# Triangle products of two RWKV blocks placed inside later projection products, and the input's sums placed behind the last gate-up low part

## Chip, cores and metric

The kernel runs on one core of a Trainium2 chip. The metric is the device time of one execution in microseconds, the median of several runs. The core has five engines with a queue each: PE (matrix products), DVE (vector), ACT (scalar and activation), POOL and SP (which here mostly issue transfers). An instruction runs when those ahead of it on its engine are issued and what it waits for on other engines is done.

## What is computed

One layer of a hybrid decoder, for 512 prompt tokens and 8 x 4 sample tokens (544 columns in all, two halves of 272). It has a half-step SwiGLU feed-forward, a mixer with 8 RWKV-7 heads beside 4 differential-attention heads, and a second half-step feed-forward, each between two RMS norms:

```python
def layer(x, l, shift0, wkv0, attend, P):
    g = P['norm_gains'][l]
    h = x + 0.5 * rms_norm(swiglu(rms_norm(x, g[0], NORM_EPS), P['ff1_in'][l], P['ff1_out'][l]), g[1], NORM_EPS)
    m, k, v, wkv, shift = mixer(rms_norm(h, g[2], NORM_EPS), l, shift0, wkv0, attend, P)
    h = h + rms_norm(m, g[3], NORM_EPS)
    h = h + 0.5 * rms_norm(swiglu(rms_norm(h, g[4], NORM_EPS), P['ff2_in'][l], P['ff2_out'][l]), g[5], NORM_EPS)
    return h, k, v, wkv, shift

def swiglu(x, w_in, w_out):
    gate, up = jnp.split(x @ w_in, 2, axis=-1)
    return (jax.nn.silu(gate) * up) @ w_out

# inside mixer, the recurrence of the RWKV heads, one step:
    sa = jnp.einsum('bhvk,bhk->bhv', S, -kk_t)
    S = (S * w_t[:, :, None, :] + sa[..., None] * (kk_t * a_t)[:, :, None, :]
         + v_t[..., None] * k_t[:, :, None, :])
    return S, jnp.einsum('bhvk,bhk->bhv', S, r_t)
```

All matrices are float32. D_MODEL is 1024, D_FF 2816, a head has 64 columns.

## The kernel before

**Precision.** Each operand is split into a high and a low part (`whi`/`wlo` for weights, `xh`/`xl` and the like for activations), and a product is three matmuls: high by high, high by low, low by high. `dot` (L153) makes one product of 128 outputs: for k = 0 to 7 the two matmuls with the weight's high part (L162, L163), then eight with its low part (L168). Three accumulation banks are taken in turn by `acc_tile` (L198): two named `mm`, one `pb`. Other banks come from `abank` (three, L190) and `bank` (two, L184), all named `pb` in the trace.

**Order.** The program is written down in one order. A planner then gives every engine its own order: it takes an instruction when it expects its inputs and its room to be ready, and among the ready ones the one written first, or one under `high_priority`. `tc.issue_after(ins)` keeps the instructions of a block that run on the engine of `ins` behind `ins`. `after(None)` (L361) does nothing. A list `norm` holds small pieces of work: `dot` takes the first one from it behind its fourth k (L164), sets it behind the matmul just made, and sets the rest of the product behind the piece's last matmul (`last[0]`, L147 to L151).

**Feed-forward.** The 22 blocks of 128 hidden columns go in four groups (`GROUPS`). In the first group, gate and up products are plain; `hidden` (L460) applies SiLU on ACT, multiplies on DVE (L462) and calls `split` (L178): the high part on ACT (L180), the low part on DVE (L181). Then `products` (L387) makes the down products, for each m first the half s = 0, then s = 1; `finish` (L624) takes each result. The other groups use seven products instead of eight for a 2x2 block product (`seven`, L520). They need sums and differences of the four quarters of the scaled input: `mixtures` (L435), 16 steps, each an addition on DVE (L440, in place in `h`), a high part on ACT (L416) and a low part on DVE (L418). In the first group `finish` takes two of these steps per result (L627), so the first eight results carry all 16. The room of `h` is then given to the weights of the next groups (`wt`, L646): their loads (`t1`, L479; `b22`, L481) wait for the last of these steps, in SP's queue, in which the down weights (L129) are loaded too.

**RWKV blocks.** After the first feed-forward, the 8 heads go in four blocks of two (L889). Block 0 has its projections from `opening`; for blocks 1 to 3, `proj` (L748) makes six products at the top of the pass: k, r and v for s = 0, then for s = 1. The passes are written one behind another, but PE's work of a projection does not depend on the blocks before it. Each block then has a chain through all engines: `gates` (L876: products L143 to L145 into abank, sigmoid L885), token shift (L826), a scan (L903), exponentials (L905, L906), the norm of kk (`sums` L207, `inv_sqrt`, `spread` L254, L918), the bonus `bon` (L926, product L929, eviction L930), the g product (L938 with L143 to L145 into abank, eviction L939 into another tile named `bon`), and the parts of `cat`, whose part 1 is L944 and part 3 is L945 and L946. The chain ends with the triangle: per chunk of 64 tokens and head the 64 x 64 product of parts 1 and 3 (L957; 16 calls, 32 matmuls in the trace, as float32 operands take two) into one abank, masked into `ltm` on DVE (L958). `cat` is then stored (L960). `ltm` of all four blocks is read by the inversion behind the loop (L971), `cat` from DRAM by `ahead` (L1032).

Of the kernel before, what the change touches and what calls it, by code (L numbers as in the profile page):

```python
# [9 lines left out]
FT = mybir.dt.float32  # L10
# [3 lines left out]
OP = mybir.AluOpType  # L14
# [3 lines left out]
DM, DFF, SEQ, NB, DT = 1024, 2816, 512, 8, 4  # L18
# [9 lines left out]
NH, HD, CH = 8, 64, 64  # L28
NCH = SEQ // CH
# [23 lines left out]
def build(ctx, tc, A):  # L53
    nc = tc.nc
    V, S, G, T = nc.vector, nc.scalar, nc.gpsimd, nc.tensor
# [52 lines left out]
    ps = pa.tile([128, 512], FT, name="pb")  # L108
# [7 lines left out]
    C = {n: cst[:, o:o + w] for n, (o, w) in CST.items()}  # L116
# [61 lines left out]
    def split(pool, src, name, n=HALF, into=None, **kw):  # L178
        hi, lo = into or [pool.tile([128, n], FR, name=name + p, **kw) for p in "hl"]
        S.activation(hi, src, AF.Copy)  # L180
        V.tensor_tensor(lo, src, hi.bitcast(FT), op=OP.subtract)  # L181
        return hi, lo

    def bank():  # L184
# [5 lines left out]
    def abank():  # L190
        return pa.tile([128, 512], FT, name="pb")
# [1 line left out]
    def xbank():  # L193
        return px.tile([128, 512], FT, name="pb")

    turn, last, latest, root = [0], [None], [None], [None]

    def acc_tile():  # L198
        turn[0] += 1
# [104 lines left out]
    later, norm, ends, got = [], [], [], [None]  # L304
# [56 lines left out]
    def after(ins):  # L361
        return ExitStack() if ins is None else tc.issue_after(ins)
# [85 lines left out]
    def ff(win, wout, pre, h, done, xp, end, lead=None, begin=None, midway=None, ahead_of_end=None):  # L448
        with ExitStack() as st:
# [5 lines left out]
            sets, scaled, mixtures = combined(pre, h, fa, xp)  # L455
# [106 lines left out]
            for gi, (j0, j1) in enumerate(GROUPS):  # L562
                if gi == 0:
                    raw = [[gate_up() for _ in range(2)] for _ in range(2)]

                    def take(s, i, ps):
                        S.activation(raw[s][i // 2][i % 2], ps, AF.Copy)

                    if lead:
                        lead(take)  # L570
                        begin()
                    else:
                        opening([weights(win[j, i], 1024) for j in range(2) for i in range(2)], pre.xs, take, 2)

                    def scaled_raw(s):
                        for g, u in raw[s]:
                            V.tensor_tensor(g, g, pre.rs[s], op=OP.mult)
                            V.tensor_tensor(u, u, pre.rs[s], op=OP.mult)
                            hidden(s, g, u)

                    scaled_raw(0)
                    behind = [None, None]
                    for j in range(2, j1, 2):
                        if midway and j == 4:
                            midway()
                        ws = [[weights(win[i, n], 1024, added=begin is None and i == 3) for n in range(2)] for i in (j, j + 1)]
                        for s in range(2):
                            for both in ws:
                                pg, pu = acc_tile(), acc_tile()
                                for p, w in zip((pg, pu), both):  # L590
                                    dot(p, w, pre.xs[s])
                                if (j, s) == (2, 0) and both is ws[0]:
                                    scaled_raw(1)
                                g, u = gate_up()
                                V.tensor_tensor(g, pg, pre.rs[s], op=OP.mult)  # L595
                                V.tensor_tensor(u, pu, pre.rs[s], op=OP.mult)
                                hidden(s, g, u)
                                with after(j > 2 and behind[0] or None):
                                    for _ in range(4 * (j > 2)):
                                        next(scaled, None)  # L600
                                behind.append(made[0])
                                behind.pop(0)
                else:
                    for j in range(j0, j1):
                        now = ahead or seven(j)
                        if ahead is None:
                            next(now)
                        ahead = None
                        next(now)
                n = j1 - j0  # L610
                lastg = gi == len(GROUPS) - 1
                sqs = [Squares(0), Squares(1)]
                if lastg:
                    st1.close()
                    xp_stack.close()
                    end()
                    st2.close()
                    late = [None, (fa, 8), (fa, 8), (pool("wx"), 4)]
                elif gi:
                    ahead = seven(j1)  # L620
                    next(ahead)
                group, hid = hid, [[], []]

                def finish(s, m, ps):  # L624
                    if gi == 0:
                        S.activation(y[s][m], ps, AF.Copy)
                        for _ in range(2):  # L627
                            next(mixtures, None)
                    else:
                        with (tc.high_priority() if lastg and m >= KB - 2 else ExitStack()):  # L630
                            V.tensor_tensor(y[s][m], ps, y[s][m], op=OP.add)  # L631
                            if lastg and m == KB - 1:
                                sqs[s].finish(y[s][m])
                            elif lastg:
                                sqs[s].add(y[s][m])
                    if lastg and m == KB - 1:
                        done(s, y, sqs[s])
                    if lastg and ahead_of_end and (s, m) == (1, 1):
                        ahead_of_end()

                products(lambda m: wout[:, m, off:off + n * 128], group, y, finish, wx=late if lastg else None, apart=lastg)
                off += n * 128
                if gi == 0:
                    next(mixtures, None)
                    h_stack.close()
                    wt = pool("wt", st1, side="right")  # L646
# [139 lines left out]
    def projected(i):  # L786

        pr = pr_.tile([128, SEQ + 1 + NB * (DT + 1)], FT, name="pr", bufs=6)
        P, Q = pr[:, :SEQ + 1], pr[:, SEQ + 1:].rearrange("p (b t) -> p b t", t=DT + 1)
        G.memset(P[:, 0:1], 0.0)  # L790
        G.tensor_copy(Q[:, :, 0:1], shin[:, i, :].rearrange("p (b o) -> p b o", o=1))

        n = SEQ - HALF

        def take(s, ps, raw=False):
            for dst, src, r in (((P[:, 1:1 + HALF], ps, 0),) if s == 0 else
                                ((P[:, 1 + HALF:], ps[:, :n], slice(0, n)), (Q[:, :, 1:], bt(ps[:, n:]), slice(n, HALF)))):
                if raw:
                    S.activation(dst, src, AF.Copy)
                else:  # L800
                    scale(s, dst, src, r)

        def scale(s, dst, src, r):
            V.tensor_tensor(dst, src, rs[0] if s == 0 else (bt if len(dst.shape) == 3 else lambda a: a)(rs[1][:, r]),
                            op=OP.mult)

        def late_scale():
            scale(0, P[:, 1:1 + HALF], P[:, 1:1 + HALF], 0)
            scale(1, P[:, 1 + HALF:], P[:, 1 + HALF:], slice(0, n))
            scale(1, Q[:, :, 1:], Q[:, :, 1:], slice(n, HALF))  # L810

        late_scales[i] = late_scale

        return (12 + i, take), (i, P, Q)
# [19 lines left out]
    def c64(ap):  # L834
        return ap.rearrange("p (c t) -> p c t", t=CH)
# [40 lines left out]
    def gates(b):  # L876
# [9 lines left out]
            out.append(t)  # L886
        return out

    for b in range(4):  # L889
        cat = pp.tile([128, NCH, 5, CH], FT, name="cat", bufs=2)  # L890
        if b:
            items, new = zip(*(projected(i) for i in (4 + b, b, 8 + b)))
            proj(*items)
            prk, prr, prv = new
        else:
            prk, prr, prv = prs[2:5]
# [53 lines left out]
        V.tensor_tensor(ars[:, b, 1], r[:, SEQ:], cu[:, SEQ:], op=OP.mult)  # L950
        V.tensor_tensor(bt(ars[:, b, 0])[:, :, 1:], bt(kk[:, SEQ:])[:, :, 1:], bt(cu[:, SEQ:])[:, :, :DT - 1], op=OP.mult)
        V.tensor_copy(bt(ars[:, b, 0])[:, :, 0:1], bt(kk[:, SEQ:])[:, :, 0:1])
        ps = abank()
        for c in range(NCH):
            for e in range(2):
                rows = slice(e * HD, (e + 1) * HD)
                T.matmul(ps[rows, c * CH:(c + 1) * CH], cat[rows, c, 1, :], cat[rows, c, 3, :], start=True, stop=True)  # L957
        V.tensor_tensor(ltm[:, b * NCH:(b + 1) * NCH], c64(ps), C["lmask"].rearrange("p (o t) -> p o t", o=1).to_broadcast([128, NCH, CH]),  # L958
                        op=OP.mult)
        nc.sync.dma_start(cat_d[b], cat)  # L960
    nc.sync.dma_start(A["shifts"], shout)
    prep.close()
    ch2 = mix.enter_context(tc.tile_pool(name="ch2", bufs=1, reuse_waits="tile"))
# [725 lines left out]
```

## Time and profile before

| | us |
|---|---|
| runs (median; lowest to highest of 3) | 1194.22 (1191.49 to 1194.61) |
| the profiled execution | 1195.87 |
| its span, first to last instruction | 1194.1 |
| mean granted clock of PE | 0.988 of full speed |

All times of the trace come from the one profiled execution. Views used: the page of the profile; the list of who waited for whom; tables of stages (busy time of PE, PEld, DVE, ACT, POOL with instruction counts, then PEclk, the share of the DMA engines and GB/s); and the order of time of single engines. A row of the order of time has the start, the time, the engine, the line, the operation, output <- inputs, shapes and a count; in brackets the idle time of the engine just before, and who ended it. PE's matmuls overlap, so the step from one start to the next says more than the time of one. The first feed-forward takes the span up to about 405 us, the RWKV projections lie between 420 and 515, attention and the recurrence up to about 755, the second feed-forward behind that.

### The profile page before, as it was taken

The numbers are of one execution on the slowest core, as the hardware profiler recorded it, in microseconds if no ns is written. First come the engines' busy times: TensorE is split into PE (matmuls) and PEld (weight loads), VectorE is DVE, ScalarE is ACT, GpSimd is POOL, SyncE is SP. The second block draws the span as 40 slices with busy tenths as digits, with TensorE's granted clock in tenths as the row PEclk, the third lists the DMA queues.
The fourth block names the chain that finished last, engine by engine and source line by source line (L and its number), as shares of the span: only waits on it lengthen the run. The fifth ranks groups of instructions, "written<-read, shape, count | busy, mean of one in ns | idle before, by whom it ended". The sixth has DMA issues, their size and how long they took to land. (4 is left out here: it accounts for less than half of the span.)

```text
span 1194.1 us, 25487 instructions
## 1 busy us (share of the span) xinstructions
PE 1169.2 (98%) x10034; PEld 1105.7 (93%) x10034; DVE 814.4 (68%) x1878; ACT 585.0 (49%) x1083; POOL 169.3 (14%) x232
## 2 busy tenths in 40 slices
PE   9999999999999999999999999999999999999995
PEld 9999999999999999989887645999999999999995
DVE  7694674865876778678335657788784766757856
ACT  7455552633645665533114545567465634525530
POOL 0001210110101176421000031100001201101001
PEclk9999999999999999899899999999999999999998
DMA  8328884975756557689442487564259876857532
GB/s 270 104 89 240 208 208 123 214 181 136 168 201 177 138 147 209 218 233 235 117 144 85 142 291 274 162 189 133 69 151 230 213 180 150 209 152 182 116 116 75
DMA packets 88330, 205.42 MB, mean 172 GB/s; under 512 B 9209, under 2 KB 22905, under 8 KB 86803
## 3 DMA queue, kind: packets, MB, share of 16 engines
q1 hardware_dynamic: 67874, 148.64, 37.7%
q0 software_dynamic: 18032, 50.70, 23.8%
q10 hardware_dynamic: 2304, 4.46, 1.0%
q8 instruction: 79, 1.29, 0.4%
q14 instruction: 41, 0.33, 0.1%
HBM read 186.12 MB, written 18.95 MB: 172 GB/s over the span
## 5 line engine op out<-in xcount | busy, mean ns | idle before, releaser
L132 ACT ACTIVATE whi<-wraw 128x1024 fp32r<-128x1024 f32 (+2 forms) x125 | 114.8, 921 | 155.8 <-PE mm L163 76.8
L162 PE MATMUL mm<-xh,whi 128*128 128x272 f32 x440 | 115.4, 293 | 0.3 <-DVE ga L595 0.3
L163 PE MATMUL mm<-xl,whi 128*128 128x272 f32 x440 | 115.0, 292 | 0.0
L138 DVE TENSOR_TENSOR wlo<-wraw,whi 128x1024 fp32r<-128x1024 f32 (+2 forms) x98 | 98.0, 1002 | 20.2 <-ACT whi L132 13.9
L483 POOL DMA_DIRECT2D t<-in_ff_in_dram x32 | 38.8, 1213 | 335.3 <-DMA t<-in_ff_in_dram 155.5
L162 PEld LDWEIGHTS mm<-xh,whi 128*128 128x128 f32 x440 | 83.6, 190 | 1.2 <-DVE ga L595 0.6
L163 PEld LDWEIGHTS mm<-xl,whi 128*128 128x128 f32 x440 | 83.6, 190 | 0.3
L529 DVE TENSOR_TENSOR ga<-pb,ga 128x272 f32<-128x272 f32 x138 | 60.2, 436 | 22.8 <-PE pb L518 20.6
L168 PE MATMUL mm<-xh,wlo 128*128 128x272 f32 x440 | 66.5, 292 | 0.3 <-DMA wlo<-in_ff_in_dram 0.3
L515 PE MATMUL pb<-sh,t1h 128*128 128x272 f32 x256 | 66.7, 288 | 0.0
L516 PE MATMUL pb<-sl,t1h 128*128 128x272 f32 x256 | 66.6, 287 | 0.0
L495 ACT ACTIVATE t1h<-t 128x1024 fp32r<-128x1024 f32 x32 | 34.0, 1062 | 60.9 <-issue 35.9
L631 DVE TENSOR_TENSOR y<-mm,y 128x272 f32<-128x272 f32 x64 | 28.2, 440 | 51.9 <-PE mm L168 51.3
L163 PE MATMUL mm<-hd0l,whi 128*128 128x272 f32 x242 | 62.7, 288 | 0.0
L162 PE MATMUL mm<-hd0h,whi 128*128 128x272 f32 x242 | 62.5, 288 | 0.0
L168 PEld LDWEIGHTS mm<-xh,wlo 128*128 128x128 f32 x440 | 59.6, 190 | 0.9 <-DMA wlo<-in_ff_in_dram 0.5
L163 PE MATMUL mm<-hd1l,whi 128*128 128x272 f32 x232 | 60.2, 288 | 0.0
L162 PE MATMUL mm<-hd1h,whi 128*128 128x272 f32 x232 | 59.9, 289 | 0.0
L162 PE MATMUL pb<-xh,whi 128*128 128x272 f32 x216 | 56.9, 294 | 0.6 <-DVE vf L1113 0.6
L163 PE MATMUL pb<-xl,whi 128*128 128x272 f32 x216 | 56.7, 292 | 0.0
L515 PE MATMUL pb<-fa,whi 128*128 128x272 f32 x216 | 56.2, 288 | 0.0
L516 PE MATMUL pb<-fa,whi 128*128 128x272 f32 x216 | 56.2, 288 | 0.0
(495 smaller groups left out, 3662.8 us busy)
## 6 DMA issues: line engine op xcount, KB each, us to landing
wraw<-in_ff_in_dram SPq DMA_DIRECT2D x55, 512.0 KB, 4.6
wlo<-in_ff_in_dram POOLq DMA_DIRECT2D x34, 512.0 KB, 7.0
t<-in_ff_in_dram SPq DMA_DIRECT2D x64, 256.0 KB, 3.8
t<-in_ff_in_dram POOLq DMA_DIRECT2D x32, 512.0 KB, 5.9
wraw<-in_w_in_dram SPq DMA_DIRECT2D x26, 512.0 KB, 7.2
wlo<-in_w_in_dram POOLq DMA_DIRECT2D x25, 512.0 KB, 8.2
wraw<-in_ff_out_dram SPq DMA_DIRECT2D x32, 384.0 KB, 3.1
wraw<-in_ff_out_dram SPq DMA_DIRECT2D x32, 320.0 KB, 3.4
```

The source lines that it names most:

```text
L132: S.activation(hi, raw, AF.Copy)
L138: V.tensor_tensor(lo, raw, hi.bitcast(FT), op=OP.subtract)
L162: T.matmul(ps, hi, xs[k][0], start=k == 0, stop=False)
L163: latest[0] = T.matmul(ps, hi, xs[k][1], start=False, stop=False).ins
L168: latest[0] = T.matmul(ps, wcols(w, k0 + k)[1], xs[k][0], start=False, stop=k == n - 1).ins
L483: G.dma_start(t1, bass.AP(tensor=src.tensor, offset=src.offset, ap=[[1024, 128], [128 * 1024 + 512, 2], [1, 512]]), accum_op=OP.add)
L495: S.activation(hi, src, AF.Copy)
L515: T.matmul(ps, c, x[k][0], start=k == 0, stop=False)
L516: T.matmul(ps, c, x[k][1], start=False, stop=False)
L529: V.tensor_tensor(dst, p, q, op=op)
L631: V.tensor_tensor(y[s][m], ps, y[s][m], op=OP.add)
```

## The change

Two independent edits.

*The sums.* `split` notes its last low part in `lowest[0]`. In the first group's `finish`, the steps taken at m = 0 (four of 16) are as before; the DVE instructions of the other 12 are set behind the last low part, which is that of the last gate-up block of the half s = 1.

*The triangles.* A block's triangle becomes `triangle(i)`, for half i of its chunks: 8 calls into an abank of its own and a mask of half the size. For blocks 2 and 3 both halves stay where the triangle was, though behind the issue of the store of `cat`. For blocks 0 and 1 they go into `hooks`, four pieces, which the pass b = 2 gives to `norm` ahead of its `proj`: so the first four of the six products of the third block's projection take one half each behind their fourth k, blocks 0, 0, 1, 1 in order.

```diff
@@ split
-        V.tensor_tensor(lo, src, hi.bitcast(FT), op=OP.subtract)
+        lowest[0] = V.tensor_tensor(lo, src, hi.bitcast(FT), op=OP.subtract).ins
@@
-    turn, last, latest, root = [0], [None], [None], [None]
+    turn, last, latest, root, lowest = [0], [None], [None], [None], [None]
@@ finish
                         S.activation(y[s][m], ps, AF.Copy)
-                        for _ in range(2):
-                            next(mixtures, None)
+                        with after(lowest[0] if m else None):
+                            for _ in range(2):
+                                next(mixtures, None)
@@ the loop over blocks
+    hooks = []
     for b in range(4):
         cat = pp.tile([128, NCH, 5, CH], FT, name="cat", bufs=2)
         if b:
+            if b > 1:
+                norm.extend(hooks)
+                hooks.clear()
             items, new = zip(*(projected(i) for i in (4 + b, b, 8 + b)))
             proj(*items)
...
-        ps = abank()
-        for c in range(NCH):
-            for e in range(2):
-                rows = slice(e * HD, (e + 1) * HD)
-                T.matmul(ps[rows, c * CH:(c + 1) * CH], cat[rows, c, 1, :], cat[rows, c, 3, :], start=True, stop=True)
-        V.tensor_tensor(ltm[:, b * NCH:(b + 1) * NCH], c64(ps), C["lmask"].rearrange("p (o t) -> p o t", o=1).to_broadcast([128, NCH, CH]),
-                        op=OP.mult)
         nc.sync.dma_start(cat_d[b], cat)
+
+        def triangle(i, b=b, cat=cat):
+
+            ps = abank()[:, :SEQ // 2]
+            cs = slice(i * NCH // 2, (i + 1) * NCH // 2)
+            for c in range(cs.start, cs.stop):
+                for e in range(2):
+                    rows = slice(e * HD, (e + 1) * HD)
+                    last[0] = T.matmul(ps[rows, (c - cs.start) * CH:(c - cs.start + 1) * CH], cat[rows, c, 1, :],
+                                       cat[rows, c, 3, :], start=True, stop=True).ins
+            V.tensor_tensor(ltm[:, b * NCH + cs.start:b * NCH + cs.stop], c64(ps),
+                            C["lmask"].rearrange("p (o t) -> p o t", o=1).to_broadcast([128, NCH // 2, CH]), op=OP.mult)
+
+        for i in range(2):
+            if b < 2:
+                hooks.append(lambda _, t=triangle, i=i: t(i))
+            else:
+                triangle(i)
```

## The prediction

> **What bounds the kernel now.** I read the page first (busy times, slices, clock), then the list of PE's waits, the table of stages in steps of 10 us, and the order of time of PE, DVE, ACT and SP round the two places that the change touches.
>
> ```profile
> span 1194.1 us, 25487 instructions
> ...
> PE 1169.2 (98%) x10034; PEld 1105.7 (93%) x10034; DVE 814.4 (68%) x1878; ACT 585.0 (49%) x1083; POOL 169.3 (14%) x232
> ...
> PEclk9999999999999999899899999999999999999998
> ```
>
> PE is busy for 98% of the span, so nearly every microsecond in which PE waits or runs at a lower clock is one of the result; DVE at 68% sets the end only where PE waits for it. The list of PE's waits (engine, tile and line <- who released it: us in all, times, longest) names these places:
>
> ```profile
> PE pb L163 <- DVE hd1l L181: 2.0, 2, 1.0
> ...
> PE pb L929 <- DVE kbs L948: 1.4, 1, 1.4
> ...
> PE pb L162 <- DVE vf L1113: 0.6, 1, 0.6
> ```
>
> The first row is the place of the second part of the change, once in each feed-forward. The other two lie right behind the RWKV blocks (516.9 and 523.0 in the order of time).
>
> **The input's sums.** Order of time of DVE, ACT, SP and PE in the first feed-forward:
>
> ```profile
> 82.80 0.78 DVE L440 TENSOR_TENSOR h<-h,h 128x272 f32<-128x272 f32 x2
> ...
> 84.91 0.43 DVE L596 TENSOR_TENSOR up<-mm,rpre 128x272 f32<-128x272 f32 x1
> ...
> 89.29 0.43 DVE L462 TENSOR_TENSOR up<-up,ga 128x272 f32<-128x272 f32 x1
> ...
> 91.41 0.43 DVE L181 TENSOR_TENSOR hd1l<-up,hd1h 128x272 fp32r<-128x272 f32 x1
> ...
> 93.24 1.97 DVE L138 TENSOR_TENSOR wlo<-wraw,whi 128x768 fp32r<-128x768 f32 x2 [1.06 <-ACT whi L132]
> ```
> ```profile
> 84.50 0.40 ACT L626 ACTIVATE y<-mm 128x272 f32<-128x272 f32 x1 [0.75 <-PE mm L168]
> ```
> ```profile
> 91.89 0.39 PE L163 MATMUL pb<-hd1l,whi 128*128 128x272 f32 x1 [1.01 <-DVE hd1l L181]
> ...
> 122.61 0.29 PE L515 MATMUL pb<-sh,t1h 128*128 128x272 f32 x1
> ```
> ```profile
> 92.21 0.33 SPq L481 DMA_DIRECT2D b<-in_ff_in_dram  x1
> ```
>
> The down product of m=0 was done before ACT emptied it at 84.50. Its 18 matmuls at 0.125 take 2.25, so the last gate-up product was done by about 82.2. DVE reached its three steps (L596, L462, L181) only at 84.91, 89.29 and 91.41, because sums (L440) and their low parts (L418) stood between; one is 0.35 (two in 0.78, overlapping by 0.08). PE waited 1.01. Of 16 sums the last 12 move behind L181: 24 DVE instructions, 8.4 us. The low part then comes some 4 to 5 us earlier, and the wait goes in both feed-forwards: **-2.0 us** (bounds 0 and -2.0; I take -2.0, as the 8.4 is much more than the 1.01). What is late next are the sums: they end near 97 instead of 92.2. Their first reader is PE at 122.61. The loads into the room of h (t1, b22, and what SP has queued behind them) start up to 5 us later. Their own factors are made with about 10 us in hand, so they cost nothing; without that cover, up to 5 each time. L138, the weights' low part, shares DVE with them, but it waits for ACT at 93.24 anyway.
>
> **The triangles: which products they go into.** In the order written down the four halves of blocks 0 and 1 go into the first four of six products of the third block's projection. PE runs far ahead of DVE there:
>
> ```profile
> 443.81 0.29 PE L162 MATMUL mm<-xh,whi 128*128 128x272 f32 x1
> ...
> 452.42 0.29 PE L162 MATMUL pb<-xh,whi 128*128 128x272 f32 x1
> ...
> 456.18 1.15 PE L957 MATMUL pb<-cat 64*64 64x64 f32 x32
> 457.26 0.39 PE L143 MATMUL pb<-twh,lora_h 64*128 64x272 f32 x1
> ...
> 470.47 1.16 PE L168 MATMUL pb<-xh,wlo 128*128 128x272 f32 x8
> 471.47 0.29 PE L162 MATMUL mm<-xh,whi 128*128 128x272 f32 x1
> ...
> 475.48 1.15 PE L957 MATMUL pb<-cat 64*64 64x64 f32 x32
> ```
> ```profile
> 454.50 0.68 DVE L944 TENSOR_TENSOR cat<-sig,pi 128x512 f32<-128x512 f32 x1
> ...
> 464.74 0.50 DVE L804 TENSOR_TENSOR pr<-mm,rpre 128x240 f32<-128x240 f32 x2
> ...
> 466.47 0.50 DVE L918 SCALAR_TENSOR_TENSOR rn<-k,vec,pb 128x272 f32<-128x272 f32 x1 [1.23 <-PE pb L254]
> 466.88 0.75 DVE L826 SCALAR_TENSOR_TENSOR k<-dif,vec,pr 128x512 f32<-128x512 f32 x1
> ...
> 471.77 0.77 DVE L926 SCALAR_TENSOR_TENSOR ksq<-r,vec,k 128x544 f32<-128x544 f32 x1
> 472.58 0.68 DVE L944 TENSOR_TENSOR cat<-sig,pi 128x512 f32<-128x512 f32 x1
> ```
>
> The third k of L826 (466.88) follows L804 of 464.74, so the third block's six products (mm, mm, pb, mm, mm, pb) are those from 443.81 to 471.47; the third starts at 452.42. A product is 24 matmuls, 3.0 us. A triangle needs cat, whose last part is L944: block 0's is there at 455.2, block 1's at 473.3. So the first product, at its fourth k at 444.8, meets a triangle whose data come 10 us later, and the third one whose data come 20 us later. In the order of before, PE did these products while it waited. Now 16 of their 24 matmuls stand behind the triangle. The three accumulation banks (two mm, one pb) are then held by waiting products, and nothing dense is left to run.
>
> **Whose bank comes first.** The halves also take abank's three banks, behind those of block 1's gates and g product:
>
> ```profile
> 438.32 0.39 PE L143 MATMUL pb<-sgh,lora_h 128*128 128x272 f32 x1
> ...
> 461.69 0.40 PE L143 MATMUL pb<-sgh,lora_h 128*128 128x272 f32 x1
> ```
> ```profile
> 455.58 0.40 ACT L930 ACTIVATE bon<-pb 128x272 f32<-128x272 f32 x1 [7.96 <-PE pb L929]
> 455.88 0.68 ACT L939 ACTIVATE bon<-pb 128x272 f32<-128x272 f32 x2
> ...
> 474.75 0.40 ACT L930 ACTIVATE bon<-pb 128x272 f32<-128x272 f32 x1 [2.02 <-PE pb L929]
> 475.05 0.68 ACT L939 ACTIVATE bon<-pb 128x272 f32<-128x272 f32 x2
> ```
>
> Block 0's g product was done at 439, yet ACT, idle for 7.96 us, emptied it only behind L930: tiles of one name are handed out in the order written. If banks are too, block 0's second half needs the bank of block 1's g product, which waits for L930, and that for L926 (471.77). So the second product too stands until block 1's chain is nearly done.
>
> **Its sum.** Block 1's chain gets shorter: its gates no longer stand behind triangle 0 (457.26 against the release at 455.9: 1.4 us), DVE is rid of the third projection's L804 and L826 (about 1.7 us), and PE answers at once (L918's 1.23 us). That is some 4 us: the banks come near 469.7, not 473.6. Left then: the rest of products 2, 3, 4 (3 x 2.0), products 5 and 6 (2 x 3.0), three halves (3 x 0.54): 13.6, so 483.3. Before, the same work (through L929 and triangle 1, 0.7 + 1.1 behind 471.47) is done at 473.3: **+10.0**.
>
> The clock, from the order of time of PE and the table of stages (PEclk is the third number from the end):
>
> ```profile
> 480.18 0.43 PE L163 MATMUL mm<-xl,whi 128*128 128x272 f32 x1
> 480.41 0.43 PE L162 MATMUL mm<-xh,whi 128*128 128x272 f32 x1
> ```
> ```profile
> 479.00:480.00 1.00, 1.00 (x8) 1.00 (x8) 1.00 (x2) 0.41 (x1) 0.00 (x0) 0.70 0.96 344
> ...
> 486.00:487.00 1.00, 1.00 (x9) 1.00 (x9) 0.32 (x1) 0.00 (x0) 0.00 (x0) 0.89 0.18 72
> ```
>
> From 479.3 to 486.1 PE has half its clock and steps of 0.23 instead of 0.125: 6.8 x (1 - 0.125/0.227) = 3.1 us lost. It follows a cluster of triangle 1, gates and small sums. I count -2.2 for it (gone in 7 of 10; bounds 0 and -3.1) and, for PE starting again after a wait of many microseconds, +2.0 (bounds 0 and 3.1, the same row). PE, late by then, also no longer waits the 1.4 and 0.6 behind the blocks, and some 0.5 of smaller waits: -2.5 (bounds 0 and -3). Triangles 2 and 3 in two halves add about 0.1 us of DVE each, beside dense products: 0. The third projection's late products hold back the next weights; their low part lands 8.2 after its issue by this row. Product 4's high part ends near 477, two copies and the issue take some 3, so it lands near 488, by my estimate 2 ahead of its reader: 0 (bound +3). The store of cat, now issued ahead of the triangle, waits for cat alone, as before: 0.
>
> ```profile
> wlo<-in_w_in_dram POOLq DMA_DIRECT2D x25, 512.0 KB, 8.2
> ```
>
> Together 10.0 + 2.0 - 2.2 - 2.5 = **+7.3** for the triangles, with the sums **+5.3**. The profiled execution took 1195.87 (its span and 1.8 round it), 1.65 above the median of 1194.22: 1201.2 by the one, 1199.5 by the other. I say 1200.
>
> The Trainium skill ("TensorE: Matmul & The Clock Gate", Part 1) says that PE's clock is halved after a window of about 3.4 us with little activity and given back after a busy one, the windows running free. The trace agrees: 6.8 us is two such windows. It speaks for the second rival below, and against this change where PE now idles longer than a window: by it the restart would cost what the cluster did, 3.1 for my 2.0, and the time would be 1201.
>
> **Rivals.**
> *Banks not in turn* (a quarter): block 0's halves run when their cat is there, at 455, and products 1, 2 and 5 are done during block 1's chain. Left at 469.5 are the rest of 3 and 4, product 6 and two halves, 8.1: 477.6, +4.3 against 473.3; with -2.2, -2.5, +1.0 for the clock and -2.0 for the sums -1.4: about 1193 to 1196, within 0.3%. For it: block 0's data are there at 455.2. Against it: the four L939.
> *The clock decides* (15 in 100): the waits at the triangles stay under 1.5 us, because DVE's chain, freed, or an order that holds the third projection back brings cat in time; then the lost 3.1 and the 2.0 of the sums are gained: -5.1, 1189 to 1191, faster. It needs cat of block 1 before PE reaches the fourth k of the third product; in the trace it is 20 us off, which is what speaks against it.
> *Late weights too* (8 in 100): the cover of 2 us fails and the half clock lasts: +10 to +13, 1205 to 1207.
> *The sums are not moved*, L181 staying late: 2 us more in each case (1 in 10).
>
> **Numbers.** The forecast has 52 in 100; the range from 1191 to 1206 leaves out part of the second rival and of the last ones. A measurement can tell about 0.3% (3.6 us) from no change. Slower by more: the forecast, the late weights, less a tail that lands under 1197.8: 0.57. Within: the quarter and that tail: 0.30. Faster: 0.13.
>
> **What would show it.** Right: PE waits of several microseconds at L957 for DVE (L944) or ACT (L939) between 445 and 470, the third block's six products ending ten microseconds later, no wait at L163 for hd1l, L440 rows behind the last L181. Wrong: third-block products running through by 472, or a half clock gone with no new wait at L957.

## The result and the profile after

The changed kernel takes 1201.15 us (median of 9 runs, 1194.95 to 1202.58), the kernel before beside it 1192.95 (9 runs, 1190.44 to 1194.83): a ratio of 1.0065 with a 95% interval of 1.0048 to 1.0081, so 5.7 to 9.7 us slower. A later comparison of the same two kernels gave 1.0056 (1.0038 to 1.0073). The profiled execution took 1201.55, against 1195.87 before: +5.68.

In the changed kernel the lines are shifted: L929 is now L934 (the bonus product), L939 is L944 (the eviction of the g product), L944 is L949 (the last part of cat), L957 is L967 (the triangle), L958 is L969 (its mask). The page of the profile after (span, PE's busy time, granted clock in 40 slices):

```profile
span 1199.8 us, 25495 instructions
...
PE 1173.1 (98%) x10034; PEld 1107.7 (92%) x10034; DVE 815.4 (68%) x1882; ACT 584.2 (49%) x1083; POOL 171.5 (14%) x232
...
PEclk9999999999999998999899999999999999999998
```

PE is as busy as before in share. The dip of the clock has moved from one slice to another, which turns out to matter. The list of PE's waits after (engine, tile, line <- who released it: us in all, times, longest):

```profile
PE pb L934 <- DVE kbs L953: 4.5, 3, 1.8
...
PE pb L254 <- DVE rx L249: 1.3, 1, 1.3
...
PE pb L143 <- ACT sig L886: 1.2, 2, 0.6
...
PE pb L162 <- DVE vf L1129: 0.5, 1, 0.5
```

The row of `hd1l` is gone: the sums did what they should. The row of `kbs` has grown from 1.4 once to 4.5 in three waits. L953 is a small DVE step just ahead of cat's last part, so this is PE waiting for a block's chain, under another name than the triangle's own.

**The sums.** Order of time of DVE after, and of PE before and after, at the first matmul behind the feed-forward:

```profile
84.74 0.44 DVE L181 TENSOR_TENSOR hd1l<-up,hd1h 128x272 fp32r<-128x272 f32 x1
85.10 1.14 DVE L440 TENSOR_TENSOR h<-h 128x272 f32<-128x272 f32 x3
...
93.88 1.50 DVE L418 TENSOR_TENSOR sl<-h,sh 128x272 fp32r<-128x272 f32 x4
```
```profile
385.52 0.29 PE L162 MATMUL pb<-xh,whi 128*128 128x272 f32 x1
```
```profile
384.24 0.29 PE L162 MATMUL pb<-xh,whi 128*128 128x272 f32 x1
```

The low part is there at 85.2 instead of 91.8, the sums end at 95.4, and the mixer starts 1.28 us earlier. The second feed-forward gains 1.27 in the same way.

**The triangles.** Order of time of PE after, in the third block's projection; then DVE and ACT:

```profile
452.97 2.15 PE L934 MATMUL pb<-ksq,cst 128*128 128x272 f32 x4 [1.28 <-DVE kbs L953]
...
458.97 1.12 PE L967 MATMUL pb<-cat 64*64 64x64 f32 x16
...
463.16 0.68 PE L967 MATMUL pb<-cat 64*64 64x64 f32 x16
...
469.43 1.16 PE L934 MATMUL pb<-ksq,cst 128*128 128x272 f32 x4 [1.78 <-DVE kbs L953]
...
472.89 1.20 PE L967 MATMUL pb<-cat 64*64 64x64 f32 x32
...
481.51 1.16 PE L168 MATMUL pb<-xh,wlo 128*128 128x272 f32 x8
```
```profile
452.89 0.68 DVE L949 TENSOR_TENSOR cat<-sig,pi 128x512 f32<-128x512 f32 x1
...
469.66 0.67 DVE L949 TENSOR_TENSOR cat<-sig,pi 128x512 f32<-128x512 f32 x1
```
```profile
470.16 0.40 ACT L935 ACTIVATE bon<-pb 128x272 f32<-128x272 f32 x1 [12.13 <-PE pb L934]
470.45 0.68 ACT L944 ACTIVATE bon<-pb 128x272 f32<-128x272 f32 x2
```

The reader should see four things. Cat of block 0 is there at 453.6 and cat of block 1 at 470.3; until then the products that carry their halves stand still at their fourth k. The third projection's last product ends at about 482.5. The first triangles come 5 and 10 us after their data, and PE is not waiting in that time: it works, but slowly. And block 0's second half (463.16) runs before block 1's g product is emptied (470.45).

Why slowly is shown by the stages (us; busy time of PE, PEld, DVE, ACT, POOL; PEclk; share of the DMA engines; GB/s), after:

```profile
452.00:455.00 3.00, 2.03 (x5) 1.59 (x6) 2.87 (x6) 0.96 (x4) 0.74 (x2) 0.50 1.06 249
455.00:458.00 3.00, 3.00 (x16) 3.00 (x15) 0.00 (x0) 2.97 (x5) 0.44 (x1) 0.50 0.95 389
458.00:461.00 3.00, 3.00 (x24) 2.63 (x25) 2.87 (x8) 0.03 (x1) 2.28 (x3) 0.50 0.45 176
...
581.00:592.00 11.00, 11.00 (x109) 9.54 (x108) 4.14 (x7) 1.34 (x3) 0.00 (x0) 0.53 0.08 26
```

After the first waits PE ran at half its clock from 452 to 462. By the steps of 0.227 against 0.125 that the prediction took from the rows before, that cost 10.2 x 0.45 = 4.6 us. The cluster with half a clock at 479 to 486 is gone. The other stages that matter are those with idle time, before and then after:

```profile
438.00:470.00 32.00, 30.32 (x257) 29.07 (x257) 25.59 (x68) 20.75 (x28) 17.81 (x32) 1.00 0.68 180
...
sum 112.00, PE 108.00 PEld 103.06 DVE 85.69 ACT 57.51 POOL 46.77; mean PE 36.00 PEld 34.35 DVE 28.56 ACT 19.17 POOL 15.59
```
```profile
438.00:470.00 32.00, 26.51 (x183) 23.82 (x182) 26.46 (x67) 13.86 (x21) 15.89 (x26) 0.84 0.59 157
...
sum 112.00, PE 104.56 PEld 97.45 DVE 79.75 ACT 54.06 POOL 46.41; mean PE 34.85 PEld 32.48 DVE 26.58 ACT 18.02 POOL 15.47
```

From 438 to 550 (the sum) PE idles 112.00 - 104.56 = 7.44 us, before 4.00. The difference arises between 438 and 470, where PE idles 5.49 against 1.68, in waits of at most 1.78.

### The profile page after: what moved, and what is told of

Same layout as the page of the kernel before. It is cut to its first block, busy times and chain, and to the rows that moved or that the text cites. A ratio compares the mean times of both kernels' runs of the same rounds, so it can differ in the third digit from the quotient of the medians.

```text
span 1199.8 us, 25495 instructions
## 1 busy us (share of the span) xinstructions
PE 1173.1 (98%) x10034; PEld 1107.7 (92%) x10034; DVE 815.4 (68%) x1882; ACT 584.2 (49%) x1083; POOL 171.5 (14%) x232
## 3 DMA queue, kind: packets, MB, share of 16 engines
q8 instruction: 79, 1.29, 0.4%
## 4 chain that ended last, share of the span: by engine, by line
PE 91%; DVE 4%; DMA 2%; issue 1%; ACT 1%; POOL 0%; SPq 0%; DVEq 0%; POOLq 0%; ACTq 0%
PE mm L162 10%; PE mm L168 10%; PE mm L163 10%; PE pb L515 7%; PE pb L516 7%; PE pb L518 7%; PE pb L162 5%; PE pb L163 5%; PE pb L168 5%; PE mm L518 3%; PE mm L516 3%; PE mm L515 3%; PE pb L1221 1%; PE pb L207 1%; PE pb L143 1%; PE pb L1063 1%
```

## The experiments

Each run states its span and mean granted clock, so a kernel's time can be parted. The *lost clock* of a run is (1 - clock) x span, and 0.9 of it is time (0.45 lost at a clock lower by 0.5, by the steps above). The *rest* is the span less that. The clock is given to three digits, so one run is uncertain by 0.5 us in it; the table has medians over a kernel's runs. *Idle* is PE's idle time from 438 to 550 in the one profile.

| kernel | median us | ratio to before (95%) | idle | lost clock | rest, against before | clock, against before |
|---|---|---|---|---|---|---|
| before (four comparisons) | 1191.1 to 1192.0 | 1 | 4.00 | 9.5 | 0 | 0 |
| the change | 1201.15 | 1.0065 (1.0048 to 1.0081) | 7.44 | 14.4 | +3.3 | +4.4 |
| change_again | 1198.14 | 1.0056 (1.0038 to 1.0073) | 7.48 | 12.0 | +3.3 | +2.2 |
| sums_only | 1189.49 | 0.9985 (0.9971 to 1.0000) | 4.56 | 8.9 | -1.5 | -0.5 |
| tri_only | 1196.41 | 1.0044 (1.0024 to 1.0065) | 6.69 | 9.6 | +4.6 | 0.0 |
| rest_free | 1193.89 | 1.0012 (0.9990 to 1.0035) | 3.86 | 10.7 | -0.1 | +1.1 |
| in_time | 1191.83 | 1.0003 (0.9987 to 1.0018) | 8.47 | 7.7 | +1.3 | -1.6 |
| halves_in_place | 1197.46 | 1.0028 (1.0005 to 1.0050) | 4.90 | 14.4 | +0.7 | +4.4 |
| whole_rest | 1196.19 | 1.0041 (1.0027 to 1.0054) | 7.65 | 10.7 | +3.3 | +1.1 |
| whole_moved | 1199.03 | 1.0060 (1.0038 to 1.0082) | 9.90 | 13.2 | +3.9 | +3.3 |
| keep_warm | 1201.97 | 1.0097 (1.0068 to 1.0125) | 6.20 | 12.0 | +9.5 | +2.2 |
| one_each | 1206.19 | 1.0100 (1.0068 to 1.0132) | 14.08 | 14.5 | +8.8 | +4.4 |
| block0_only | 1203.99 | 1.0117 (1.0088 to 1.0146) | 12.34 | 15.6 | +7.4 | +5.5 |
| block1_only | 1206.64 | 1.0129 (1.0105 to 1.0152) | 14.11 | 16.9 | +9.1 | +6.6 |

The change itself is set against the mean of the four of before (rest 1181.8, lost clock 9.5). The profile of in_time is that of one of its slowest executions (1200.07), so its idle time stands for that one alone. So the loss has two parts of like size: 3.3 us of rest, in which the gain of the sums is already contained, and 2.2 to 4.4 us of clock. The parting is arithmetic on medians: it says how much goes with the clock, and not why the clock fell.

**The change again, and each edit alone.** First the unchanged copy, as a base within the second comparison.

> The changed kernel itself once more, on the chip of the next three. Theory (PE's waits and the half clock behind them, with the clock's windows falling differently in each run): 5 to 9 us above the kernel before. Rival (the first measurement was high by its chip; the parts add up): the triangles alone gave +5.3 and the sums alone -1.6, so +3.7 or less.

Then the sums without the triangles (the triangles as before), and the triangles without the sums:

```diff
-                        with after(lowest[0] if m else None):
+                        with after(None):
```

> The sums behind the last low part alone, triangles as before. Theory: the two waits at hd1l go and nothing else is late; PE was 1.28 us earlier behind the first feed-forward and 1.27 behind the second, so 2.5 us under the kernel before (-2.0 to -3.0). Rival: the gain is given back where the RWKV chain or a half clock sets the time, then -1 or less.

> The triangles in the third block's products alone, sums as before. Theory (PE waits for cat and then runs at half clock): 8.2 + 2.5 = about 10.7 us above the kernel before (9 to 12). Rival (the two parts work on each other, the earlier first feed-forward moving the clock's windows): about 8.

The change came out as expected the second time, +6.5 by medians. The sums alone gain 1.6 us by medians (interval: 0 to 3.5), between the two expectations. The triangles alone lose 5.3 (2.9 to 7.7), less than either expectation. The two together, +3.7, are less than the change's +6.5 to +8.2, and the table says where: tri_only has about the change's rest and what the sums gained (4.6 against 3.3 + 1.5), but none of its clock. Why the clock falls with both edits, and not with the triangles alone, no run shows. In tri_only's profile half the clock holds from 455 to 463 (3.42 of lost clock where the change lost 5.12), and nowhere in the recurrence.

**The rest of a product set free.** The triangle still follows the fourth k, but the product no longer follows the triangle:

```diff
                     last[0] = T.matmul(ps[rows, (c - cs.start) * CH:(c - cs.start + 1) * CH], cat[rows, c, 1, :],
                                        cat[rows, c, 3, :], start=True, stop=True).ins
+            last[0] = None
```

> The changed kernel, but the rest of a product no longer stands behind the triangle that is set into it (the triangle still follows the fourth k). The theory that the loss is what stands behind the waiting triangle (16 of 24 matmuls of a product, and through three such products all the work behind): the products of the third projection run on, PE's idle between 438 and 470 falls from 5.5 us to about 2.6 us, the end of the third projection comes within 2 us of the place that it has with the triangles in halves at their old place, and the time falls by 2 us or more, to a ratio of 1.003 or less, as with the halves in place (1.0028) or better. The rival that the loss lies in the halves and in the blocks' own chain: the ratio stays at 1.0045 to 1.007 with idle of 5 us.

This is the run that names the cause of the rest. The last product of its third projection, then its stages and its waits in the mixer:

```profile
470.78 1.16 PE L168 MATMUL pb<-xh,wlo 128*128 128x272 f32 x8
```

```profile
438.00:470.00 32.00, 30.71 (x251) 28.62 (x251) 25.60 (x69) 19.93 (x28) 17.95 (x32) 1.00 0.68 179
...
sum 112.00, PE 108.14 PEld 101.25 DVE 85.44 ACT 56.54 POOL 46.04; mean PE 36.05 PEld 33.75 DVE 28.48 ACT 18.85 POOL 15.35
```
```profile
PE pb L934 <- DVE kbs L953: 1.4, 1, 1.4
...
PE pb L143 <- DVE ltm L970: 0.6, 1, 0.6
```

The third projection ends at 471.8, where the change had 482.5 and the kernel before 471.5. The idle time between 438 and 470 is 1.29 instead of 5.49, the clock there is full (the half clock lies at 482 to 488, near where before had it), only one wait for `kbs` is left (the one of before), and the time is 1.0012 of before. The triangles, their halves and their banks are all still there. So 5 to 6 us (1.0056 and 1.0065 against 1.0012) go when nothing stands behind the triangle: 3.4 of them are rest (+3.3 to -0.1), which is the cost of the products that waited. The others are clock, and there the cause is less sure: halves_in_place below loses as much clock as the change with no product waiting, and tri_only, where products wait, loses none. Nor is all of the loss gone: rest_free is still 0.0027, about 3 us, above sums_only, 1.4 of it rest; the two intervals just overlap.

**Halves where their data are.** Block 0's halves in the last two products of the third projection, block 1's in the third and fourth of the next:

```diff
-                norm.extend(hooks)
-                hooks.clear()
+                norm.extend([0] * (4 if b == 2 else 2) + hooks[:2])
+                del hooks[:2]
```

(a 0 lets a product pass without a piece.)

> All of the change, but block 0's halves in the last two of the third block's six products and block 1's in the third and fourth of the fourth block's, where cat is there. Theory (waiting is what costs): no wait at the triangles, no half clock between 450 and 465; the time is that of the sums alone, 2.5 us under the kernel before, or up to 3.1 less again if the half clock at 479 goes too. Rival (the halves cost by themselves: more instructions, more banks, products cut in two): still 3 us or more above the sums alone.

1.0003 of before: the loss is gone, and so is the gain of the sums. PE has no wait at the triangles and no half clock between 450 and 465, as the theory said; but the time lies 2.1 us above sums_only by the ratios (the intervals overlap), between the two expectations. The waits of its one profile between 500 and 560 show what was late there, the chain of the last block:

```profile
PE mm L162 <- DVE q_f L1132: 1.8, 1, 1.8
PE pb L937 <- DVE kbs L956: 1.7, 1, 1.7
PE pb L1066 <- DMA ar<-cat_d: 1.7, 1, 1.7
```

So even at a place where the data are ready, a move of the triangles out of the chain is not shown to have bought anything here.

**Halves, at the old place.** No hooks; all four triangles in halves, each with its own bank:

```diff
-            if b < 2:
+            if b < 0:
```

> The sums moved, and all four triangles in halves with a bank each where they stood, none in a product. Theory (the place costs, not the halves): as the sums alone, -1.6 (-0.5 to -3). Rival (two banks and twice the mask instructions delay the next block's gates): 1.5 us or more above the sums alone, so at or over the kernel before.

The ratio is 1.0028, 0.0043 above sums_only, so, as the rival said, the halves with their banks are not free even where the triangle was. The times fall into two groups: four runs from 1191.76 to 1193.35 with clocks of 0.992 and 0.993, eight from 1195.28 to 1201.73 with 0.991 down to 0.987. The rest is 2.2 us above sums_only; which step of the halves costs that is not shown. The greater part of the difference is clock. Stages of this kernel, then of sums_only:

```profile
462.00:472.00 10.00, 10.00 (x44) 9.00 (x43) 5.10 (x17) 5.51 (x7) 3.58 (x6) 0.53 0.11 40
```
```profile
462.00:472.00 10.00, 10.00 (x73) 10.00 (x73) 8.13 (x20) 5.72 (x8) 5.24 (x7) 0.86 0.19 55
```

PE is busy all the time in both; one has 44 matmuls done at a clock of 0.53, the other 73 at 0.86.

**The last two blocks whole.** The change, but the triangles of blocks 2 and 3 in one bank as before (`triangle` takes the number of parts):

```diff
-        for i in range(2):
-            if b < 2:
-                hooks.append(lambda _, t=triangle, i=i: t(i))
-            else:
-                triangle(i)
+        if b in (0, 1):
+            for i in range(2):
+                hooks.append(lambda _, t=triangle, i=i: t(i, 2))
+        else:
+            for i in range(1):
+                triangle(i, 1)
```

> The changed kernel with the triangles of the third and fourth block whole in one bank as before; the halves of the first two stay in the products. If the prediction's zero for those halves holds: no difference from the changed kernel, ratio to before 1.0056, range 1.004 to 1.0075. The rival from the run with all halves at their old place: four groups of 16 in place of two of 32 cost 0.16 us each on PE (0.62 to the next matmul against 1.08 for two), so 0.3 us, and two banks instead of one are held by each triangle, so that the gates behind them come later and the clock falls: 1.5 to 3 us faster than the changed kernel, ratio about 1.003 to 1.004.

1.0041, 1.8 us under change_again by the ratios, with overlapping intervals: on the edge of both expectations. The rest is +3.3 as in the change; what differs is clock (10.7 against 12.0). The halves of blocks 2 and 3 cost no work that can be seen here; whether they cost clock stays open.

**Whole triangles moved.** Blocks 0 and 1 each as one piece, behind the fourth k of the first and second product of the third projection (not of the next projection of each block, as the expectation has it). Against the run before:

```diff
         if b in (0, 1):
-            for i in range(2):
-                hooks.append(lambda _, t=triangle, i=i: t(i, 2))
+            for i in range(1):
+                hooks.append(lambda _, t=triangle, i=i: t(i, 1))
```

> Sums moved; the triangles of the first two blocks whole, each behind the fourth k of the first product of the next projection; the others whole in place. Theory 1, the place makes the loss (the data of block 0 are not ready when the first product reaches its fourth k): nearly as slow as the changed kernel, 4 to 7 us over before, ratio 1.0035 to 1.006, with one wait of PE for cat or for kbs before 460 and an idle of about 5 us of PE between 438 and 470 as with halves. Theory 2, the halves and their banks make it: about the time of the kernel that only moves the sums, ratio 0.998 to 1.0005, idle about 2.5 us.

1.0060: in a product, whole triangles lose as much as halves. But PE's long wait here is another than I wrote, 4.08 for weights, which the change does not have and the next two runs do. So this run does not part the place from the halves in the change itself; rest_free does.

**One block alone, and one block for each projection.** Only block 0's halves in products, then only block 1's, each with the other triangles whole where they stood (both edits against whole_rest); and, against the change, block 0's in the first two products of the third projection with block 1's in the first two of the fourth:

```diff
-        if b in (0, 1):
+        if b in (0,):
```
```diff
-        if b in (0, 1):
+        if b in (1,):
```
```diff
-                norm.extend(hooks)
-                hooks.clear()
+                norm.extend(hooks[:2])
+                del hooks[:2]
```

> Sums moved; only the first block's triangle set in halves inside products, all others whole in place. By the place theory the loss is made in the third projection, where the first half waits for its cat data while they are being written: 3 to 6 us over before, ratio 1.0025 to 1.005, near the changed kernel; by the rival that both blocks share the loss, half of it: 1 to 2 us over before, ratio 1.001 to 1.0017.

> Sums moved; only the second block's triangle set in halves inside the fourth projection, all others whole in place. In the changed kernel block 1's halves ran together 3 us after its cat was done, so by the place theory little is lost here: 0 to 1.5 us over the kernel that moves the sums alone, ratio 0.998 to 1.000. By the rival that both blocks share the loss: 1 to 2 us over before, ratio 1.001 to 1.0017.

> Block 0's halves in the first two products of the third block's projection, as changed, but block 1's in the first two of the fourth block's, one projection after its own turn. Theory (both blocks' waits count, block 1's more, as two products and a bank stand until 470): about half of the loss goes, +1 to +4 against the kernel before, with the wait for L934 of block 1 at 469 gone and that of block 0 at 453 still there. Rival (the first wait alone, with the half clock it brings on, makes the loss): +6 to +8 as changed.

All three expectations failed: each is slower than the whole change, by 5 to 9 us against change_again by the ratios. (One of them also named the wrong place: pass b = 2 takes whatever is in the list, so block 1's halves went into the first two products of the third projection, not of the fourth.) Order of time of PE in sums_only, whole_moved, block0_only and block1_only:

```profile
454.11 0.77 PE L168 MATMUL pb<-xh,wlo 128*128 128x272 f32 x4 [0.84 <-DMA wlo<-in_w_in_dram]
```
```profile
454.42 1.87 PE L168 MATMUL pb<-xh,wlo 128*128 128x272 f32 x7 [4.08 <-DMA wlo<-in_w_in_dram]
```
```profile
454.07 1.80 PE L168 MATMUL pb<-xh,wlo 128*128 128x272 f32 x8 [3.38 <-DMA wlo<-in_w_in_dram]
...
474.53 1.67 PE L934 MATMUL pb<-ksq,cst 128*128 128x272 f32 x4 [4.84 <-DVE kbs L953]
476.13 3.17 PE L967 MATMUL pb<-cat 64*64 64x64 f32 x64
```
```profile
454.69 2.18 PE L168 MATMUL pb<-xh,wlo 128*128 128x272 f32 x8 [4.59 <-DMA wlo<-in_w_in_dram]
...
478.41 2.15 PE L934 MATMUL pb<-ksq,cst 128*128 128x272 f32 x4 [5.01 <-DVE kbs L953]
480.49 1.12 PE L967 MATMUL pb<-cat 64*64 64x64 f32 x16
```

The weights' low part of the third product lands at about 454 in every one of them. Where only the first two products carry a piece, the third is free, so it is PE's next dense work: PE comes to its low part some 4 us before it is there, and waits 3.4 to 4.6 for it in whole_moved, block0_only and block1_only (one_each waits 3.2 there, and 4.3 more for weights later on). In the change the third product stands at its own piece, and this wait is not met. After that, in block0_only and block1_only, the two `mm` banks are still held, the one `pb` bank has served both its products, and PE waits another 4.8 or 5.0 for block 1's chain with nothing dense left. So the effects of the four pieces do not add up: to take two of them away unblocks a product that the weights are not ready for. In block0_only PE's order also has block 0's halves behind block 1's L934, 20 us after their data; why the planner put them there was not settled.

**The clock held up.** In the change, 24 matmuls with a weight of zeros ahead of the third piece, where PE has little to do:

```diff
             if k == 3 and norm and not rest:
+                if keep:
+                    for _ in range(keep.pop(0)):
+                        with after(latest[0]):
+                            latest[0] = T.matmul(ps, zero, xs[k][0], start=False, stop=False).ins
```

> The changed kernel with 24 more matmuls by a zero weight in the third of the products that wait, ahead of its triangle: 3 us of dense work that adds nothing, in time in which PE waits anyway. Theory that the half clock from 452 to 462 is a large part (10.2 us x 0.45 = 4.6): 3 to 4.6 us under the changed kernel, so +4 to +5 against the kernel before. Rival that the missing data alone cost (PE would reach the same waits sooner): as the changed kernel, +8, within 1 us.

The theory failed: 1.0097. (`keep` holds 0, 0, 24.) In its order of time of PE the filler is met twice, the second time in the second feed-forward, where nothing hides it:

```profile
450.91 3.27 PE L172 MATMUL pb<-xh,zero 128*128 128x272 f32 x24
...
832.89 3.20 PE L172 MATMUL mm<-xh,zero 128*128 128x272 f32 x24
```

The list of fillers was filled in two passes, so 3.2 us of the result belong to the experiment and not to the question. The first set was not hidden either: the change's rest of 3.3 and twice 3.2 make 9.7, and the table has 9.5. What it was to buy did not come: its lost clock is that of change_again (12.0), and in its profile half the clock holds from 446 to 450 and from 459 to 467, the latter 5 us behind the filler. Less the second set, the time is about 8 us over before, which is what the rival said. Nothing here shows that the clock can be bought back so.

## Why the prediction was right, and where not

**The sums: right.** -2.0 was said; the trace has -1.28 and -1.27 (-2.6), the timed kernel -1.6 with an interval that reaches from 0 to -3.5. The trace's gain lies beyond my bound of -2.0: the waits of 1.01 were a little less than what they cost. The low part came 6.7 us earlier, where I had 4 to 5. The sums delayed nothing: they end at 95.4, as forecast near 97, with their first reader at 121.3.

**The products that meet unwritten data: right, and the cause of the rest.** This was the core of the forecast: 16 of 24 matmuls stand behind a triangle whose data come 10 and 20 us later. rest_free takes that one thing away, and with it go the idle time (5.49 to 1.29), the 11 us by which the third projection ended later, and 3.4 us of rest; the half clock at 452 and the other 1 to 3 us went with it, but that they must is not shown. The sign that I had named did not come: no wait of several microseconds at the triangle's line. PE waits at most 1.78 at a time between 438 and 470, for the chain's `kbs`, since its order has other work ahead of the triangles; much of the delay is work at half clock.

**Whose bank comes first: wrong.** I had block 0's second half wait until block 1's g product is emptied. It ran at 463.16, that eviction at 470.45. Product 2 was therefore finished earlier than I said. This was the rival with banks not in turn, which I had put at a quarter, and its time did not come either, because it let products 1, 2 and 5 run at full speed while block 1's chain ran. They had half the clock instead.

**Its sum: near, with other parts.** The chain of block 1 released PE at 469.43, against "near 469.7"; as the sums start everything 1.28 earlier, the chain itself took 1 us longer than I had said. Left were 80 dense matmuls (10.0; I had 12.0) and about 3 us of triangle, bonus products and gates, so the last product ends at 482.5. The forecast was 483.3, with the restart's 2.0 and the sums' -1.0 484.3. The restart did not come on top of it: the half clock lay before 469.43, beside block 1's chain, where it held up products 1 and 2, and product 5 (3.0), which the rival had done by then, was still to do. That the half clock is why is argued from these rows, not shown by a run.

**The clock: its size was wrong.** The restart was put at +2.0 with a bound of 3.1; it took 4.6 in the profile, three windows of about 3.4 us instead of two. Before's cluster, put at -2.2, did go (-3.1). Over the runs of each kernel the clock cost the change 2.2 to 4.4 us in all, where the forecast had -0.2. The Trainium skill ("TensorE: Matmul & The Clock Gate", Part 1) gives 3413 ns for the window and speaks of an idle window as the trigger. Its length agrees: the stretches between 450 and 490 lose 1.71 us of clock in sums_only, 3.42 in before and 5.12 in the change, halves of one, two and three windows. The trigger is not seen so in the records. In the 3.41 us ahead of the fall at 451.9 PE was busy 2.04, with 11 matmuls, where a dense stretch of that length holds 27; in the 3.41 us ahead of before's fall at 479.3 it was busy throughout, with triangle, gates and small sums.

**The later waits: wrong in part.** I had PE, late by then, no longer wait the 1.4 and 0.6 behind the blocks. Both are still there (1.42 at 523.25 for `kbs`, 0.53 for `vf`): what comes later on PE also makes the chain later that PE waits for.

**Blocks 2 and 3: 0 holds for the work**, as whole_rest's rest shows; its clock is open. But the sum has no term for halves as such, and halves_in_place has 2.2 of rest above sums_only. **Late weights: 0 held in the change.** Where the third product is free, its own low part is late by 3.4 to 4.6, which I had not priced.

So the time, 1200 against 1201.15, was right, with the main cause of the rest. Its parts were not: without the clock 10.0 - 2.0 - 2.5 = +5.5 was forecast and +3.3 came, and the clock, forecast at -0.2, brought 2.2 to 4.4 more. The difference from before came out larger than the forecast +5.3 (+7.7 by the ratio, +6.7 in the second comparison), while the kernel before ran at 1192.95 and not at the 1194 to 1196 that I had counted from. That these made up for each other in the time is luck.

None of the kernels is shown to be faster than the kernel before; sums_only, the best, has an interval that ends at 1.0000.

## What to carry to other kernels

Work that is set into a product with the product's rest behind it must have its data ready when the engine that runs ahead gets there, and not when the chain would want it: look for the time of the data first, then choose the product, or let the product go on without it. When a step is set to wait, count the accumulation banks that the waiting products hold, and ask which product is next when they are taken, and whether its weights are there. With 98% of PE busy, read the granted clock beside the idle time: here each made about half of the loss.

## What was not expected of the hardware

Half clock holds while the records show PE busy without a pause: 11.00 of 11 us from 581 to 592 in the recurrence (clock 0.53), and 10.00 of 10 from 462 to 472 in halves_in_place. It also sets in after such a stretch: in halves_in_place PE was busy all of the 3.4 us from 457.5 to 460.9, and at 461.1 the clock fell. What it takes to make it fall is not shown. In these profiles it comes in multiples of 3.41 us (3.41 in sums_only at 461, 6.83 in before, 10.24 in the change, 20.48 in in_time), and how many an execution meets varies: the 28 runs of before in the first comparison have clocks from 0.988 to 0.995 and spans from 1187.2 to 1194.9. Most of the spread of this kernel's times goes with it, as the two groups of halves_in_place show, so that one profile is not enough to say where a kernel loses its clock.
